# Sixty-four bytes of padding at the end of SBUF: where the right-hand tiles of an encoder layer begin

## The chip, the cores and the metric

The kernel runs on one core of a Trainium2 chip. A core has TensorE (PE in the profile, with its weight loads as PEld), VectorE (DVE), ScalarE (ACT), GpSimd (POOL) and SyncE (SP, which issues nearly all DMAs here). The engines work on SBUF, a memory of 128 partitions; TensorE writes its sums to PSUM. The metric is the device time of one execution in microseconds (us), the median over several runs.

## The reference, cut to what matters

One layer of a bidirectional encoder over 2048 tokens of width 1024, in float32:

```
h = rms_norm(x);  z = h @ w_in
y_a = mLSTM heads (chunks of 128, forward and backward scans) of z
y_b = latent attention, 4 heads, softmax over all 2048 keys, of z
x = x + concat(y_a, y_b) @ w_out
x = x + square(relu(rms_norm(x) @ w_ff1)) @ w_ff2        # 1024 -> 4096 -> 1024
```

## The kernel before

**Matmuls in three parts.** A float32 operand is split into a high and a low part of type float32r (names end in h and l), and a product is the sum of high x high, high x low and low x high. `mm3` (lines 68 to 71) issues these three matmuls. The first operand given to a matmul is the stationary one, loaded into TensorE before it; the second is the moving one, streamed through. The profile prints a matmul as out<-moving,stationary.

**Stages.** `phase_a` computes the norm, the input projection and what follows from it, and stores it to DRAM; a planner orders its instructions. From then on the order is written out by hand, and each engine runs its instructions in the order of the program:

- `attention` (line 989): blocks of 256 queries; for each half block and each 512 keys, a score group of five matmuls (lines 1075 to 1079), then softmax, transposes of the probabilities (line 1120) and the products with the values. The steps of the mLSTM are woven in between. `out` (line 1143) normalises a block into the tile y and stores it.
- `OutProj` (line 1288): the product with w_out, whose weights lie in the tiles woh0, wol0 and so on, with y as the stationary operand in ring tiles.
- `FeedForward` (line 1450). The first layer, `layer1`, uses a Strassen-like scheme: for each of 32 units (16 slices f of the hidden width, for each of 2 halves of the tokens), 7 products p of 12 matmuls each. `product` gives `mm3` the W1 combination wh, wl as the stationary operand, and the token combination `H[p]` as the moving one. The second layer, `layer2`, works in the same way with products pd.

**Where tiles lie.** Pools of tiles are taken from the left end of SBUF upwards, or with `side="right"` from the right end downwards; a pool that is closed gives its place to the next one. What matters here:

- Right, in this order from the end: `y_out` (line 998), which holds the one tile y; `stage` with eight raw tiles; then, in attention, the keys and queries (`k_sb`, `q_sb`), and in their place later `ring` (line 1315, tiles r), `o_w` (line 1316, the woh and wol), `f_h1` (the token combinations h3 to h6), and for the second layer `g_r` and `g_acc`.
- Left: the constants, the probabilities p, their transposes, the values, mLSTM tiles, later `f_h0` (the token combinations h0 to h2), `f_raw1` (W1 tiles w1raw) and the operands of the second layer.

All of these tiles but y and small ones of the mLSTM have a size that is a multiple of 128 bytes in each partition. So the size of y, which is opened first at the right end, sets where all the later right-hand tiles begin relative to such multiples.

**Which tiles a product meets.** For products 0 to 2 of units 1 to 11, `w1_split` (line 1497) puts the stationary W1 part into the left-hand w1raw tiles; in all other cases it goes into the right-hand ring:

```
if 0 < n < self.LOW and op < 3 and (n, op) != (1, 2):
    w = self.r1p.tile([P, 2, 4, P], F32R, name=f"w1raw{self.nlow % 2}")
else:
    w = self.ring.pool.tile([P, 2, 4, P], F32R, name="r0" if n or 2 < op < 6 else "r1")
```

The tokens of the first half are h0 to h6, for products 0 to 6. For the second half, `exchange` (line 1550) puts the tokens of product 0 into stage tiles (raw), those of product 1 into ring tiles (r), and those of products 2 to 6 into the places of h0 to h4.

Of the kernel before, what the change touches and what calls it, by code (L numbers as in the profile page):

```python
# [8 lines left out]
F32 = mybir.dt.float32  # L9
# [9 lines left out]
P = 128  # L19
# [969 lines left out]
def attention(c, keep, drain, project):  # L989

    nc, tc = c.nc, c.tc
    with ExitStack() as st:
        ent = st.enter_context
        skq, sl = ExitStack(), ExitStack()
        def pool(name, bufs, side="left", ent=ent, **kw):
            return ent(tc.tile_pool(name=name, bufs=bufs, side=side, reuse_waits="tile", **kw))

        op = pool("y_out", 1, "right", keep.enter_context)
# [143 lines left out]

        def out(b):
            h, blk = divmod(b, NB)
            y = op.tile([P, 264], F32, name="y")[:, 0:256]
            nc.vector.tensor_tensor(y, pvs.pop(b), dens.pop(b), op=ALU.mult)

            def store():
                nc.sync.dma_start(c.d_yb[h, :, blk * 256:(blk + 1) * 256], y)
            return store  # L1150
# [21 lines left out]
        for g in range(8 * N):  # L1172
# [4 lines left out]
            if r >= 0 and r % 8 == 6 and r // 8 < N:  # L1177
                out(r // 8)()
# [61 lines left out]
        invert(b)  # L1240
        transpose_group(b, 2, 0)
        out(b - 1)()
        transpose_group(b, 1, 1, True)
        pv(b, 0)
# [10 lines left out]
        next(after)  # L1255
        pv(b, 3)
        store = out(b)
        for _ in after:
            pass
# [751 lines left out]
```

## Time and profile before

| | us |
|---|---|
| median of 3 runs | 2583.69 (2583.47 to 2584.41) |
| profiled execution, first to last instruction | 2586.2 |
| TensorE busy in it | 2567.1 (99%) |
| VectorE | 1679.2 (65%) |
| ScalarE | 1211.0 (47%) |
| GpSimd | 402.9 (16%) |

No other time is given for the profiled execution than its span. In the span, `phase_a` takes about the first 460 us, attention with the mLSTM lasts until about 1155, the out-projection until 1348, the first feed-forward layer until 1972, and the second one until the end. A matmul is pipelined: a record lasts longer than the distance to the next one's start, so TensorE's rate is read from starts, and its busy share doesn't tell the rate.

### The profile page before, as it was taken

To read this page: it belongs to the slowest core of one execution; us is meant where nothing else is said; L and a number is where in the kernel's file an instruction comes from. 1 tells how busy PE (TensorE), PEld (TensorE's weight loads), DVE (VectorE), ACT (ScalarE), POOL (GpSimd) and SP (SyncE) were. 2 spreads that over 40 slices of the span, in tenths; PEclk is the share of its full clock that TensorE was granted. 3 is DMA by queue.
4 is the path that set the end of the run, shared out by engine and by line. 5 is a ranking of instruction groups with operands and counts; after the bars stand their busy time and mean duration, and the time that the engine had idled before them with its cause. 6 is when DMAs were issued, how large, how long until landed. Compare 5 with 4: busy or idle time off the path is not lost. (4 is left out here: it accounts for less than half of the span.)

```text
span 2586.2 us, 37106 instructions
## 1 busy us (share of the span) xinstructions
PE 2567.1 (99%) x13232; PEld 2170.3 (84%) x13232; DVE 1679.2 (65%) x3206; ACT 1211.0 (47%) x2457; POOL 402.9 (16%) x438
## 2 busy tenths in 40 slices
PE   9999999999999999999999999999999999999999
PEld 7888888888888888898888888888888888888887
DVE  5585467666676667675448777877775577676443
ACT  5454444546656566561135554655554323332332
POOL 1211111023224224121000000000000233232000
PEclk9999999999999999999999999999999999999999
DMA  5434234356455555336675655744446644444652
GB/s 172 144 118 143 91 119 145 81 137 133 96 95 122 88 119 96 88 109 185 200 242 174 200 192 191 255 167 143 163 142 250 242 144 146 147 147 147 211 177 96
DMA packets 297757, 391.57 MB, mean 151 GB/s; under 512 B 32677, under 2 KB 186340, under 8 KB 297572
## 3 DMA queue, kind: packets, MB, share of 16 engines
q1 hardware_dynamic: 295108, 384.74, 49.7%
q10 hardware_dynamic: 2464, 4.46, 0.5%
q8 instruction: 104, 1.70, 0.3%
q14 instruction: 81, 0.66, 0.1%
HBM read 256.94 MB, written 132.17 MB: 150 GB/s over the span
## 5 line engine op out<-in xcount | busy, mean ns | idle before, releaser
L69 PE MATMUL pd<-w2h,uh 128*128 128x512 f32 x896 | 348.7, 389 | 0.1
L71 PE MATMUL pd<-w2h,ul 128*128 128x512 f32 x896 | 348.6, 389 | 0.0
L70 PE MATMUL pd<-w2l,uh 128*128 128x512 f32 x896 | 348.5, 389 | 0.0
L54 DVE TENSOR_TENSOR ul<-ur,uh 128x1024 fp32r<-128x1024 f32 x110 | 144.4, 1312 | 248.7 <-ACT uh L53 248.4
L53 ACT CAST uh<-ur 128x1024 fp32r<-128x1024 f32 x110 | 115.9, 1054 | 395.5 <-PE pd L70 381.0
L54 DVE TENSOR_TENSOR ptl<-ptp,pth 128x512 fp32r<-128x512 f32 x252 | 173.5, 689 | 171.5 <-ACT pth L53 166.5
L53 ACT CAST pth<-ptp 128x512 fp32r<-128x512 f32 x252 | 146.3, 582 | 244.9 <-PE ptp L1120 228.6
L1629 DVE TENSOR_TENSOR e<-pu,e 128x512 f32<-128x512 f32 x224 | 151.0, 687 | 96.0 <-PE pu L71 94.0
L1080 DVE TENSOR_SCALAR_CACHE_REDUCE p<-ps 128x512 f32<-128x512 f32 x256 | 174.6, 682 | 53.5 <-PE ps L1079 42.6
L69 PEld LDWEIGHTS pd<-w2h,uh 128*128 128x128 f32 x896 | 168.2, 188 | 35.4 <-DVE e L1629 0.5
L71 PEld LDWEIGHTS pd<-w2h,ul 128*128 128x128 f32 x896 | 168.2, 188 | 35.0
L70 PEld LDWEIGHTS pd<-w2l,uh 128*128 128x128 f32 x896 | 168.2, 188 | 34.9
L1789 POOL TENSOR_TENSOR r<-wr,r 128x512 f32<-128x512 f32 x48 | 92.2, 1920 | 614.5 <-DMA wr<-in_w 599.2
L1120 PE MATMUL ptp<-ident,p 128*128 128x128 f32 x1008 | 151.3, 273 | 0.7 <-ACT p L1091 0.7
L69 PE MATMUL pz<-wh,hh 128*128 128x512 f32 (+1 forms) x384 | 149.9, 392 | 2.1 <-ACT hh L53 1.1
L71 PE MATMUL pz<-wh,hl 128*128 128x512 f32 (+1 forms) x384 | 150.3, 391 | 0.0
L70 PE MATMUL pz<-wl,hh 128*128 128x512 f32 (+1 forms) x384 | 149.7, 391 | 0.1
L70 PE MATMUL pv<-ptl,vh 128*128 128x256 f32 x496 | 140.8, 284 | 2.3 <-DVE ptl L54 1.9
L69 PE MATMUL pv<-pth,vh 128*128 128x256 f32 x496 | 140.6, 284 | 0.4 <-ACT pth L53 0.4
L71 PE MATMUL pv<-pth,vl 128*128 128x256 f32 x496 | 140.3, 283 | 0.0
L1632 ACT ACTIVATE e<-e 128x512 f32<-128x512 f32 x128 | 81.0, 633 | 124.0 <-DVE e L1629 117.2
L1091 ACT ACTIVATE p<-p,nm 128x2048 f32<-128x2048 f32 x64 | 128.6, 2009 | 20.8 <-DVE nm L1084 20.2
(470 smaller groups left out, 6561.8 us busy)
## 6 DMA issues: line engine op xcount, KB each, us to landing
d_u<-e SPq DMA_DIRECT2D x224, 256.0 KB
ur<-d_u SPq DMA_DIRECT2D x110, 512.0 KB
wr<-in_w SPq DMA_DIRECT2D x96, 256.0 KB
w1raw<-in_w SPq DMA_DIRECT2D x42, 512.0 KB
raw<-in_w_in SPq DMA_DIRECT2D x48, 256.0 KB
r<-in_w SPq DMA_DIRECT2D x22, 512.0 KB
mb<-d_M SPq DMA_DIRECT2D x32, 256.0 KB
r<-in_x SPq DMA_DIRECT2D x16, 512.0 KB
```

Source lines behind the costliest of these rows:

```text
L53: r = nc.scalar.copy(hi, src)
L54: (eng or nc.vector).tensor_tensor(lo, src, hi.bitcast(F32), op=ALU.subtract)
L69: nc.tensor.matmul(out, ah, bh, start=first, stop=False)
L70: nc.tensor.matmul(out, ah, bl, start=False, stop=False)
L71: nc.tensor.matmul(out, al, bh, start=False, stop=last)
L1080: nc.vector.tensor_scalar(probs[b, a][:, j, :], o, SCALE, None, op0=ALU.mult, op1=ALU.max, accum_out=maxes[b, a][:, j:j + 1])
L1091: nc.scalar.activation(p, p, AF.Exp, bias=maxes.pop((b, a)), accum_out=dens[b][:, a:a + 1])
L1120: nc.tensor.transpose(pt[:, k, :], p[:, j, k * P:(k + 1) * P], c.ident)
L1629: nc.vector.tensor_tensor(out, o, t, op=ALU.add)
L1632: nc.scalar.activation(t, t, AF.Relu)
L1789: nc.gpsimd.tensor_tensor(R, wr, R, op=ALU.subtract)
```

## The change

The tile y of an output block has 256 columns that are used and a padding behind them. The padding grows from 8 to 24 columns of 4 bytes:

```diff
         def out(b):
             h, blk = divmod(b, NB)
-            y = op.tile([P, 264], F32, name="y")[:, 0:256]
+            y = op.tile([P, 280], F32, name="y")[:, 0:256]
             nc.vector.tensor_tensor(y, pvs.pop(b), dens.pop(b), op=ALU.mult)
```

All right-hand tiles opened from then on begin 64 bytes further down in each partition, on multiples of 128 bytes. The instructions stay as they are.

## The prediction

> **What bounds the kernel now.** I read the page first, then TensorE's waits, then the stretches of the feed-forward layers, and then the matmuls one product at a time.
>
> ```profile
> span 2586.2 us, 37106 instructions
> ...
> PE 2567.1 (99%) x13232; PEld 2170.3 (84%) x13232; DVE 1679.2 (65%) x3206; ACT 1211.0 (47%) x2457; POOL 402.9 (16%) x438
> ```
>
> TensorE (PE) is busy for 2567.1 of 2586.2 us. Its longest wait is the first load of the kernel, and it is not touched here:
>
> ```profile
> PE pt L204 <- DMA rows<-in_g_mix: 4.6, 1, 4.6
> ```
>
> So the time is the sum of the matmuls' spacings, and a change to addresses can matter only if it changes a spacing or opens a wait. Busy time doesn't show spacings, because a matmul's record overlaps the next one. The stretches below are the first feed-forward layer in two halves (us; then PE, PEld, DVE, ACT, POOL busy with counts, clock, DMA share, GB/s):
>
> ```profile
> 1348.00:1660.00 312.00, 311.48 (x1398) 256.55 (x1397) 255.06 (x417) 168.04 (x302) 9.28 (x24) 1.00 0.62 203
> 1660.00:1972.00 312.00, 311.74 (x1358) 253.99 (x1357) 234.28 (x365) 166.71 (x269) 0.00 (x0) 1.00 0.47 158
> ```
>
> The granted clock is 1.00 in both, VectorE works 234.28/312 = 75% of the second, and the DMA engines 47%.
>
> The next view groups the matmuls of line 69, the first of the three in `mm3`. A name reads out<-moving,stationary; the three times are min/median/max of one matmul's duration in ns.
>
> ```profile
> L69 PE MATMUL pd<-w2h,uh x896: 389/389/494, 1971.9 to 2580.9; 128*128 128x512 f32 x180
> L69 PE MATMUL pv<-pth,vh x496: 277/283/384, 479.8 to 1149.1; 128*128 128x256 f32 x166
> ...
> L69 PE MATMUL po<-woh,r x256: 389/389/481, 1158.9 to 1347.2; 128*128 128x512 f32 x128
> ...
> L69 PE MATMUL pu<-h3h,r x128: 388/389/476, 1356.4 to 1968.5; 128*128 128x512 f32 x128
> L69 PE MATMUL pu<-h4h,r x128: 387/389/475, 1359.9 to 1971.3; 128*128 128x512 f32 x128
> L69 PE MATMUL pu<-h2h,r x88: 392/394/398, 1353.5 to 1965.8; 128*128 128x512 f32 x88
> L69 PE MATMUL pu<-h0h,r x84: 394/394/394, 1347.9 to 1960.2; 128*128 128x512 f32 x84
> L69 PE MATMUL pu<-h1h,r x84: 394/394/394, 1350.7 to 1963.0; 128*128 128x512 f32 x84
> L69 PE MATMUL pm<-wuqh,cTh x64: 334/337/343, 59.9 to 421.1; 128*128 128x384 f32 x64
> ...
> L69 PE MATMUL pu<-r,r x64: 389/389/389, 1665.3 to 1957.4; 128*128 128x512 f32 x64
> L69 PE MATMUL pu<-h0h,w1raw x44: 389/389/476, 1368.1 to 1566.5; 128*128 128x512 f32 x44
> ```
>
> Matmuls of one shape have two durations, and the odd ones are h0, h1 and h2 against the ring tile r: 394 ns instead of 389. Set the operands' places beside it. By the tile sizes in the code, h0 to h2 lie on the left side, on multiples of 128 bytes. The ring, h3 to h6 and the stage tiles lie on the right side, which now sits 64 bytes off such multiples. The same h0 against the left-hand w1raw takes 389; a right-hand moving tile (h3h, h4h, r) against the ring takes 389; pd, left against left, takes 389. So **both operands at the same distance from a multiple of 128 is the fast case; 0 against 64 is the slow one**.
>
> What it is worth is read from the timeline of one unit f of the second half, at the first matmul of a product (12 matmuls each):
>
> ```profile
> 1743.05 0.39 PE L69 MATMUL pu<-r,r 128*128 128x512 f32 x1
> ...
> 1745.77 0.39 PE L69 MATMUL pu<-h0h,r 128*128 128x512 f32 x1
> ...
> 1754.17 0.39 PE L69 MATMUL pu<-h3h,r 128*128 128x512 f32 x1
> ...
> 1756.91 0.39 PE L69 MATMUL pu<-h4h,r 128*128 128x512 f32 x1
> ```
>
> The product r,r takes 1745.77 - 1743.05 = 2.72 us (227 ns a matmul). The three products h0, h1, h2 take 8.40, which is 2.80 each (233 ns). The product h3 behind them takes 2.74: it needs 0.02 to find the fast rhythm again.
>
> **The change part by part.** The padded row grows from 264 x 4 = 1056 = 8 x 128 + 32 bytes to 280 x 4 = 1120 = 8 x 128 + 96. All right-hand tiles opened after it move down by 64 bytes, onto multiples of 128. No instruction, DMA or byte moved is added or taken away; nothing reads the padding.
>
> *1. The mismatched products, the main term.* The ring holds the stationary operand of h0, h1, h2 for 88 + 84 + 84 = 256 matmuls of line 69, and a product has four of these: 64 products. Each goes from 2.80 to 2.72 if all operands then sit at distance 0: 64 x 0.08 = **5.12 us**.
>
> *2. The products behind a change of distance.* h3 follows a mismatched product in units 12 to 31 (from 12 on, all W1 tiles come from the ring): 20 x 0.02 = **0.40 us**. In units 1 to 11 most of h0 to h2 go against w1raw, left against left, and h3 then changes over to right against right:
>
> ```profile
> 1550.84 0.39 PE L69 MATMUL pu<-h2h,w1raw 128*128 128x512 f32 x1
> ...
> 1553.56 0.39 PE L69 MATMUL pu<-h3h,r 128*128 128x512 f32 x1
> ...
> 1556.33 0.39 PE L69 MATMUL pu<-h4h,r 128*128 128x512 f32 x1
> ```
>
> h2 takes 2.72 and h3 2.77 here: 11 x 0.05 = 0.55, of which I take **0.50**, because the starts are rounded to 0.01.
>
> *3. Attention.* Keys and queries are both on the right and keep equal distances. But each score group stands between left-hand work (transposes of p, pv), so its edges change.
>
> ```profile
> 802.36 0.48 PE L1075 MATMUL ps<-kh,qh 128*128 128x512 f32 x1
> ...
> 803.37 0.39 PE L1079 MATMUL ps<-rl,qr 128*128 128x512 f32 x1
> ```
>
> Four matmuls take 1.01 us. There are 256 groups. The lower bound of the cost: the four matmuls behind the first come down from about 233 ns (the mismatched spacing) to 227, 4 x 0.0067 x 256 = 6.8 us gained. The upper bound: they lose a changeover of 0.01 (half of h3's 0.02), 256 x 0.01 = 2.6 us lost. The operands of a score match before and after, so I take **0**, and keep both ends.
>
> *4. What produces W1.* A unit of the second half then takes 7 x 2.72 = 19.04 us instead of 3 x 2.80 + 3 x 2.72 + 2.74 = 19.30. VectorE needs 75% of 19.30 = 14.5 us in it, ScalarE 53% = 10.3, so neither becomes the bound, and the matmuls hide them as before. Their own speed doesn't depend on the side:
>
> ```profile
> L47 DVE TENSOR_TENSOR r<-r,r 128x512 fp32r<-128x512 f32 x35 | 23.9, 684 | 1.1 <-ACT r L1505 1.1
> ...
> L47 DVE TENSOR_TENSOR w1raw<-r,w1raw 128x512 fp32r<-128x512 f32 x20 | 13.7, 683 | 0.0
> ```
>
> A row all on the right takes 684 ns, one across the sides 683: **0**. With no cover, 1 ns on each of the 365 VectorE operations of the second half would be 0.4 us. GpSimd does nothing in the second half.
>
> *5. Waits.* The 64 bytes move tile edges against tiles of earlier pools. By the sizes in the code, two edges that touched a weight slice of the opening stage no longer do, and the projection weight woh5 now touches the end of one mLSTM tile num1. It would wait for the last reader of num1:
>
> ```profile
> 1140.33 0.30 ACT L896 ACTIVATE num<-num 128x128 f32<-128x128 f32 x1
> L53 ACT CAST woh<-r x8: 627/632/637, 1159.0 to 1162.6; 128x512 fp32r<-128x512 f32 x8
> ```
>
> That ends at 1140.63, and the first cast from the ring, of which woh5 is one, comes at 1159.0: 18 us of cover, **0**. With the cover gone, whatever is late at ScalarE there delays the out-projection one for one.
>
> Sum: 5.12 + 0.40 + 0.50 = **6.0 us**. The profiled span is 2586.2, which is 2.5 above the runs' median of 2583.69; the profile has that on top, and the gain lies in spacings of an engine that never rests, so it comes off both: 2580.2 for the span and **2577.7 us** for the runs.
>
> **The rivals.**
>
> *No change (2583.7).* The 5 ns may belong to the sides being different, not to the 64 bytes. For it: every slow row has left moving and right stationary, and before shows no cross pair with equal distances in a long run. Against it: h3 lies right beside h2 and is fast, with the same ring; nothing but a 64-byte step is known to lie between them. The Trainium skill, TensorE: Matmul & The Clock Gate, section "Step-by-step: what each phase is for", speaks for this rival: TensorE has two independent read ports, so loading the next weights doesn't steal read bandwidth from the running matmul, and where operands lie could not matter. The trace disagrees with it so far: 394 against 389 ns.
>
> *Slower: the moving tile's own distance counts, wherever the stationary one is on the right.* h0 at 0 is slow and h3 at 64 fast against the same ring, which this explains as well as I do. Then h0 to h2 stay at 2.80, and the 128 fast ring products (of 224 products, 32 go against w1raw and 64 are slow already) and the out-projection (256 x 3 / 12 = 64 groups of twelve) all go to 2.80: (128 + 64) x 0.08 = 15.4 us, **2599.1**. It decides from 65 such groups on (65 x 0.08 = 5.2). Against it: wuqh with cTh, both on the right and on multiples of 128. From pd and pv a column costs (389 - 283)/256 = 0.41 ns, so 384 columns should take 389 - 53 = 336 in the fast class and 341 in the slow one; it takes 337.
>
> *Only the products (2578.6).* The changeovers stay, as they come from changing tiles: 2583.7 - 5.1.
>
> *Attention too (2570.9).* Step 3 at its lower bound, 2577.7 - 6.8.
>
> **How the numbers follow.** Chances: my forecast 0.66, only the products 0.10, attention too 0.08, no change 0.11, slower 0.05. A measurement of this kernel can tell about 0.2% (5.2 us) from no change. The forecast lies 0.8 us beyond that bound, "only the products" on it: I give it 0.03 faster, 0.07 same. Faster: 0.65 + 0.03 + 0.08 = 0.76; same: 0.11 + 0.07 = 0.18; slower 0.06 with what is left. The range takes in the forecast with some microseconds of step 3 to either side, and "only the products": 2573.0 to 2581.0. It leaves out no change, slower, and the far end of attention, about 0.2.
>
> **What would show it.** In the profile after: h0h,r to h2h,r at 389 ns like h3h,r, and a unit of the second half at 19.04 us (step 1); h3 at 2.72 in all units (step 2); score groups at 1.01 (step 3); VectorE and ScalarE rows of line 47 and 1505 unchanged (step 4); no new wait of TensorE near 1160 us (step 5). The forecast falls if h0h,r still shows 394, or if h3h,r or po rises to 394.

## The result, and the profile after

The changed kernel takes 2576.55 us (median of 9 runs, 2573.88 to 2577.52), the kernel before 2583.69 (9 runs): a ratio of 0.9971, with a 95% interval of 0.9962 to 0.9981. That is 7.1 us, where 6.0 were forecast. Instructions and counts are the same.

```profile
span 2575.0 us, 37106 instructions
...
PE 2557.5 (99%) x13232; PEld 2169.6 (84%) x13232; DVE 1675.9 (65%) x3206; ACT 1210.3 (47%) x2457; POOL 393.3 (15%) x438
```

The two profiled spans differ by 11.2 us, more than the medians. The execution profiled before lay some 4 us above the median of the runs: a span here is 1.8 us shorter than the device time of its execution (2576.82 for 2575.0), so 2586.2 stands for about 2588. I therefore compare stages, and take totals from the ratios.

The first feed-forward layer, in the view of the matmuls of line 69 (min/median/max ns, first and last start):

```profile
L69 PE MATMUL pu<-h3h,r x128: 387/389/476, 1350.4 to 1957.4; 128*128 128x512 f32 x128
L69 PE MATMUL pu<-h4h,r x128: 388/389/476, 1354.2 to 1960.1; 128*128 128x512 f32 x128
L69 PE MATMUL pu<-h2h,r x88: 389/389/389, 1347.6 to 1954.7; 128*128 128x512 f32 x88
L69 PE MATMUL pu<-h0h,r x84: 389/389/389, 1342.2 to 1949.2; 128*128 128x512 f32 x84
L69 PE MATMUL pu<-h1h,r x84: 389/389/389, 1344.9 to 1951.9; 128*128 128x512 f32 x84
```

The 394 ns of h0, h1 and h2 have become 389. In the timeline, the same unit as shown of before:

```profile
1737.73 0.39 PE L69 MATMUL pu<-h0h,r 128*128 128x512 f32 x1
...
1745.89 0.39 PE L69 MATMUL pu<-h3h,r 128*128 128x512 f32 x1
...
1748.61 0.39 PE L69 MATMUL pu<-h4h,r 128*128 128x512 f32 x1
```

The three products take 8.16 us, 2.72 each, and the h3 behind them 2.72 too. From the first matmul of this layer to the first of the next, the layer now takes 1960.8 - 1342.2 = 618.6 us. Before, it took 1971.9 - 1347.9 = 624.0.

That is 5.4 us, not 6.0, because two waits of this layer grew:

```profile
PE pu L71 <- DVE r L47: 0.7, 1, 0.7
...
PE pu L70 <- DVE h4l L47: 0.6, 1, 0.6
```

They were 0.5 and 0.3 before. With the slower start behind them (the timeline shows h3 of unit 0 at 3.77 us against 3.55 before, and h4 of unit 16 at 3.65 against 3.27) they give back 0.6 us. TensorE seems to come to them earlier than VectorE can deliver.

Attention gained as well, which I had not counted. Before, by the groups of the score matmuls (busy us, mean ns of one):

```profile
L1078 PE MATMUL ps<-rh,qr 128*128 128x512 f32 x256 | 101.6, 397 | 0.0
...
L1079 PE MATMUL ps<-rl,qr 128*128 128x512 f32 x256 | 101.3, 396 | 0.0
```

and after:

```profile
L1078 PE MATMUL ps<-rh,qr 128*128 128x512 f32 x256 | 100.9, 394 | 0.0
L1079 PE MATMUL ps<-rl,qr 128*128 128x512 f32 x256 | 100.5, 392 | 0.0
```

The records of the last two matmuls of a group are 3 and 4 ns shorter. What attention gained by it is tried below, with kq192.

### The profile page after: what moved, and what is told of

Its sections match the earlier page's. It is cut to its first block, busy times and chain, and to the rows that moved or that the text cites. A ratio compares the mean times of both kernels' runs of the same rounds, so it can differ in the third digit from the quotient of the medians.

```text
span 2575.0 us, 37106 instructions
## 1 busy us (share of the span) xinstructions
PE 2557.5 (99%) x13232; PEld 2169.6 (84%) x13232; DVE 1675.9 (65%) x3206; ACT 1210.3 (47%) x2457; POOL 393.3 (15%) x438
## 5 line engine op out<-in xcount | busy, mean ns | idle before, releaser
L1789 POOL TENSOR_TENSOR r<-wr,r 128x512 f32<-128x512 f32 x48 | 82.8, 1725 | 619.1 <-DMA wr<-in_w 599.1
```

What stands on the lines that cost most here:

```text
L1789: nc.gpsimd.tensor_tensor(R, wr, R, op=ALU.subtract)
```

## The experiments

My theory, A: a matmul pays 6.7 ns when its moving and its own stationary tile begin at different places modulo 128. Its rivals were B, that multiples of 128 are fast wherever the other operand lies, and C, that moving tile edges, and not alignment, did it. In each run the sum of the three products h0 to h2 against the ring in one unit of the second half (unit 20 of before and after, 21 of the others) tells what a slow product costs: 8.40 us before, 8.16 after. Ratios are against the kernel before, run on the same chip.

**left64: the old padding, the left side moved instead.**

```diff
-        c.e = ep.tile([P, 12, 512], F32, name="e")
+        c.e = ep.tile([P, 12 * 512 + 16], F32, name="e")[:, 0:12 * 512].rearrange("p (a n) -> p a n", a=12)
```

> Padding as before (264 columns), but 64 bytes of padding behind the left-hand tile e, so that h0 to h2, the w1raw tiles and the second layer's operands begin 64 bytes off multiples of 128, as the right-hand tiles do. Theory A (a matmul pays 6.7 ns when its moving and its own stationary tile begin at different places modulo 128): every product of the first feed-forward layer takes 2.72 us, as after, and the changeovers vanish; about 6.0 us faster than before, near 2577.7; attention stays as before. Theory B (multiples of 128 are what is fast, wherever the other operand lies): h0 to h2 against the ring stay at 2.80, and h0 to h2 against w1raw and all of pd may join them; no gain or a loss, 2583.7 or more.

Ratio 0.9977 (0.9968 to 0.9987).

```profile
1761.32 0.39 PE L69 MATMUL pu<-h0h,r 128*128 128x512 f32 x1
...
1769.48 0.39 PE L69 MATMUL pu<-h3h,r 128*128 128x512 f32 x1
```

8.16 us: all products are fast with every tile of these products 64 bytes off a multiple of 128. B falls, and so does the reading that the multiples themselves are what the change brings. The layer takes 618.5 us, as after. The ratio alone tells less: its interval, 3.4 to 8.3 us, holds the expected 6.0 and the 7.1 of the change.

**both: the new padding and the left side moved.** The edit of left64 on the changed kernel, so that left and right lie 64 bytes apart again, the other way round.

> Padding as after (280 columns) and the 64 bytes behind e as well: right-hand tiles on multiples of 128, left-hand feed-forward tiles 64 off. Theory A: the slow products come back, h0 to h2 against the ring at 2.80 us, 64 x 0.08 + 0.9 = 6.0 us slower than after, near 2582.5; the gain of attention stays. Theory B: the ring and h3 to h6 are on multiples of 128, so they are fast; h0 to h2 are off them, so they are slow both against the ring and against w1raw: 96 products at 2.80. The rows tell the two apart: h0h against w1raw takes 389 ns by A and 394 by B.

Ratio 0.9986 (0.9977 to 0.9995).

```profile
1759.90 0.40 PE L69 MATMUL pu<-h0h,r 128*128 128x512 f32 x1
...
1768.16 0.40 PE L69 MATMUL pu<-h3h,r 128*128 128x512 f32 x1
...
1770.93 0.39 PE L69 MATMUL pu<-h4h,r 128*128 128x512 f32 x1
```

```profile
L69 PE MATMUL pu<-h0h,w1raw x44: 389/394/477, 1363.9 to 1562.3; 128*128 128x512 f32 x44
L69 PE MATMUL pu<-h1h,w1raw x44: 389/389/476, 1366.6 to 1565.0; 128*128 128x512 f32 x44
```

By the sign set beforehand, h0h against w1raw at 394 would speak for B. But B has all of h0 to h2 slow against w1raw, and h1h takes 389: left against left is fast, and h0h is the first product after a change of sides. Left against right is slow again, but costs less: 8.26 us for three products instead of 8.40, and 2.77 for the h3 behind. A forecast 8.40. It has no place for this: 0 against 64 and 64 against 0 are the same distance modulo 128.

**pad272 and pad256: right-hand tiles 32 and 96 off.**

```diff
-            y = op.tile([P, 280], F32, name="y")[:, 0:256]
+            y = op.tile([P, 272], F32, name="y")[:, 0:256]
```

(256 in the second.)

> 272 columns: all right-hand tiles 32 bytes off multiples of 128, left-hand ones on them. Theory A in its strict form (any difference costs the same): h0 to h2 against the ring at 2.80 us, as before, near 2583.7. Theory A with 64-byte halves (only the 64 counts): 2.72 us, near 2576.6 as after. A cost that grows with the distance would give about 2.76 us, near 2580. Theory C (what the change did was to move tile edges, not alignment) expects a time anywhere between.

> 256 columns, no padding: all right-hand tiles 96 bytes off multiples of 128, that is 32 below them, left-hand ones on them. Theory A in its strict form: 2.80 us for h0 to h2 against the ring, near 2583.7. With 64-byte halves: 96 counts as 64, 2.80 us, near 2583.7. With the distance to the nearest multiple of 128 counting: as for 272 columns.

Ratios 0.9992 (0.9983 to 1.0001) and 0.9998 (0.9989 to 1.0007).

```profile
1763.09 0.40 PE L69 MATMUL pu<-h0h,r 128*128 128x512 f32 x1
...
1771.49 0.39 PE L69 MATMUL pu<-h3h,r 128*128 128x512 f32 x1
```

```profile
1765.28 0.40 PE L69 MATMUL pu<-h0h,r 128*128 128x512 f32 x1
...
1773.71 0.40 PE L69 MATMUL pu<-h3h,r 128*128 128x512 f32 x1
```

8.40 and 8.43 us: the whole price for 32 as for 96. It neither grows with the distance nor comes in halves of 64.

**pad296 and pad312: further down.** These separate places modulo 128 (A1) from the signed distance over a longer stretch (A2).

```diff
-            y = op.tile([P, 280], F32, name="y")[:, 0:256]
+            y = op.tile([P, 296], F32, name="y")[:, 0:256]
```

(312 in the second.)

> 296 columns: right-hand tiles once more 64 bytes off multiples of 128, but 128 bytes further down than in before. Theory A1 (the places modulo 128 decide, moving at 0 and stationary at 64 being the dear order and moving at 64 with stationary at 0 the cheaper one): h0 to h2 against the ring at 2.80 us as before, ratio near 1.000. Theory A2 (the signed distance over a longer stretch, modulo 256, decides: the moving tile began 64 below the stationary one in before and 64 above it in both, and here it is 64 above it): 2.76, 2.75, 2.75 and 2.77 us for h0, h1, h2 and the h3 behind them, as in both, ratio near 0.999. Theory C (tile edges or room): neither of the two patterns.

> 312 columns: right-hand tiles on multiples of 128 as after, but 128 bytes further down, so that left and right differ by 128 modulo 256. Theory A1: everything as after, all products at 2.72 us, ratio near 0.997. Theory A2: a distance of 128 is a distance like another, h0 to h2 against the ring above 2.72.

Ratios 0.9982 (0.9973 to 0.9991) and 0.9986 (0.9977 to 0.9995).

```profile
1766.63 0.40 PE L69 MATMUL pu<-h0h,r 128*128 128x512 f32 x1
...
1774.89 0.40 PE L69 MATMUL pu<-h3h,r 128*128 128x512 f32 x1
```

```profile
1767.16 0.40 PE L69 MATMUL pu<-h0h,r 128*128 128x512 f32 x1
...
1775.56 0.39 PE L69 MATMUL pu<-h3h,r 128*128 128x512 f32 x1
```

With 296 columns the right side lies 64 off multiples of 128, just as in before, and yet the three products take 8.26 us as in both. With 312, **every tile of these products lies on a multiple of 128 and they are slow again, 8.40 us**. A1 falls twice; A2 stands. C falls too: the patterns follow the distances.

**pad344 and pad288: how long is the stretch, and does the sign count?** The same edit with 344 and 288 columns.

> 344 columns: right-hand tiles 256 bytes further down than after. Theory A2 (the signed distance of the moving tile's begin from the stationary one's decides, modulo some length; 0 is the only fast one so far, and 128 is slow): if the length is 256, every product takes 2.72 us again, ratio near 0.997. If it is 512 (the step between two slices of a stationary tile, so it cannot be longer), 256 is one more slow distance, h0 to h2 against the ring above 2.72, ratio near 0.999.

> 288 columns: right-hand tiles 32 bytes further down than after, the moving tiles h0 to h2 begin 32 above the stationary ones (modulo 256). Theory A2: plus 64 cost 2.75 to 2.77 us, minus 32 cost 2.80. If the sign is what makes the difference, plus 32 lies between 2.72 and 2.77, ratio near 0.998. If every distance but plus 64 costs the same, 2.80, ratio near 1.000.

Ratios 0.9978 (0.9968 to 0.9987) and 0.9993 (0.9984 to 1.0002).

```profile
1760.75 0.39 PE L69 MATMUL pu<-h0h,r 128*128 128x512 f32 x1
...
1768.91 0.39 PE L69 MATMUL pu<-h3h,r 128*128 128x512 f32 x1
```

```profile
1763.24 0.40 PE L69 MATMUL pu<-h0h,r 128*128 128x512 f32 x1
...
1771.64 0.40 PE L69 MATMUL pu<-h3h,r 128*128 128x512 f32 x1
```

With 256 more bytes the products are fast, 8.16 us: the stretch is 256. With a distance of 32 in the other direction they cost 8.40, so the sign alone doesn't make a product cheap; plus 64 is the one distance tried that is cheaper. Together, with places from the layout of the program:

| moving (left) minus stationary (right), modulo 256 | three products, us | from |
|---|---|---|
| 0 | 8.16 | after, left64, pad344 |
| +32 | 8.40 | pad288 |
| +64 | 8.26 | both, pad296 |
| 128 | 8.40, 8.39 | pad312, ident64 |
| -96 | 8.43 | pad256 |
| -64 | 8.40 | before |
| -32 | 8.40 | pad272 |

**kq64 and kq192: attention's share.** Both are the changed kernel with a gap that moves only keys and queries.

```diff
         rp = pool("stage", 8, "right", keep.enter_context)
+        pool("gap", 1, "right", skq.enter_context).tile([P, 48], F32, name="gap")
         kp = pool("k_sb", 5, "right", skq.enter_context)
```

(16 columns in kq64.)

> Padding as after (280 columns), but 64 bytes of padding between the stage tiles and the keys and queries, so that only keys and queries lie 64 bytes off again, as in before; all of the feed-forward layers as after. If keys and queries on multiples of 128 are what shortens attention, the score groups go back to their spacings of before (the four matmuls behind the first 1.3 + 0.7 + 0.5 us in total longer) and the time is about 2 us longer than after, ratio near 0.998. If attention's share in the gain is chance (waits of one execution), the time is that of after, ratio near 0.997.

kq64 has a ratio of 0.9972 (0.9961 to 0.9984), as the changed kernel, and its last two score rows show 394 and 393 ns, as after. By its expectation attention's share would be chance. But by the stretch of 256 it hadn't restored the old places: keys and queries lay 64 below the left side's places, not 64 above them. Hence kq192, with the changed kernel once more beside it (again):

> Padding as after, and 192 bytes between the stage tiles and the keys and queries, which puts these at the same places modulo 256 as in before; all else as after. If attention's share of the gain comes from where keys and queries lie, the matmuls behind the first of a score group go back to their spacings of before, and the time is about 2 us above that of the same kernel without the gap, in the run beside it. If not, both agree within 0.5 us.

> The changed kernel once more, beside the others, as what kq192 is compared with: ratio near 0.997, attention's score groups as in the profile after.

kq192 takes 2583.34 us (0.9983, 0.9975 to 0.9992) and the changed kernel 2580.98 (0.9973, 0.9963 to 0.9982). That is 2.4 us. The intervals overlap, but 9 of the 11 executions of kq192 took longer than every one of the 9 of the changed kernel. The score groups of kq192, one line number higher, are those of before, 397 and 396 ns:

```profile
L1079 PE MATMUL ps<-rh,qr 128*128 128x512 f32 x256 | 101.6, 397 | 0.0
L1080 PE MATMUL ps<-rl,qr 128*128 128x512 f32 x256 | 101.3, 396 | 0.0
```

and those of the changed kernel beside it are short again:

```profile
L1078 PE MATMUL ps<-rh,qr 128*128 128x512 f32 x256 | 101.0, 395 | 0.0
L1079 PE MATMUL ps<-rl,qr 128*128 128x512 f32 x256 | 100.4, 392 | 0.0
```

Records don't tell the rate, so I add up the distances from start to start of the 1280 score matmuls, short waits included: 324.3 us in kq192 against 322.3 in again, and 323.6 in before against 321.3 in after. That is 2.0 and 2.3 us. The whole stretch from the first score to the first projection matmul can't be used for this. It takes 713.0 us in kq192 and 710.7 in again, which looks like the difference of the medians, but 707.2 in after, which is the same kernel as again: waits there differ by some microseconds from one execution to the next. So attention's share follows where keys and queries lie, and its size, about 2 us, is less sure than that of the feed-forward layer. The two placements that differ by 128 bytes, kq64 and kq192, do not act alike here either.

**ident64: can the transposes' settling be shortened?** After transposes, matmuls take 231 to 236 ns for a while before they run at 227. Here the identity, their moving operand, moves by 64 bytes on the changed kernel:

```diff
-    c.ident = pool.tile([P, P], F32, name="ident")
+    c.ident = pool.tile([P, P + 32], F32, name="ident")[:, 16:P + 16]
```

> Padding as after, but the identity matrix, the moving operand of all transposes, lies 64 bytes off a multiple of 128, and everything on the left side behind it 128 bytes higher. Theory A1: the feed-forward products stay at 2.72 us; the transposes have moving at 64 and stationary at 0. If the distance also sets how long the matmuls behind transposes take to settle (231 to 236 ns instead of 227 for up to ten matmuls), the score groups change by up to 0.02 us each, 5 us in all, either way; if it does not, the time is that of after.

Ratio 0.9987 (0.9978 to 0.9996), slower than the changed kernel.

```profile
1766.82 0.40 PE L69 MATMUL pu<-h0h,r 128*128 128x512 f32 x1
...
1775.21 0.39 PE L69 MATMUL pu<-h3h,r 128*128 128x512 f32 x1
```

The loss is in the feed-forward layer: the left side moved by 128 with the identity, and the three products take 8.39 us, as in pad312. So A1 falls here a third time. The four score rows behind the first of a group show 394 to 395 ns, against 392 to 396 after: nothing was won there. No version tried beats the changed kernel.

## Why the prediction was right or wrong

*Direction and size were right*: 7.1 us (4.9 to 9.8 by the interval) against 6.0, the time 1.1 below the forecast and inside the range. That the total came so near is helped by two terms taken as 0, attention's gain and the waits of step 4, which went opposite ways.

*Step 1, the mismatched products*: as forecast, 8.40 to 8.16 us for three, 64 products by 0.08. In the traces these 64 took 179.2 us before and 174.2 after. left64 shows it without the change: matching the sides from the left gives the same product times.

*Step 2, the changeovers*: as forecast. h3 takes 2.72 after h2, where it took 2.74.

*Step 3, attention, taken as 0*: this is the term that was mis-sized. It is about 2 us gained (2.4 by the medians of kq192 and the changed kernel, 2.0 to 2.3 by the starts), inside the bounds of 6.8 gained and 2.6 lost. The step named the left-hand work around a group but took it for nothing, because the operands of a score match before and after. In the traces the matmuls behind the first of a group lie 232 to 236 ns apart in the median before and 230 to 233 after, not at the steady 227. That what stands around so short a group sets this is inferred; only the place of keys and queries was tried. Why some matmuls of a group gain and others don't was not shown.

*Step 4, taken as 0*: 0.6 us was given back, though neither VectorE nor ScalarE became the bound of a unit. The two waits were short before (0.5 and 0.3 us) and belong to single places, the weights of unit 0 and h4 for the second half; a mean load of 75% doesn't show them. That their suppliers kept their pace while TensorE came sooner is inferred, not tried by itself. It fits that left64, which speeds up the same products in another way, shows the same waits, 0.7 and 0.6 us.

*Step 5, waits from moved edges*: no wait of TensorE above 0.15 us in the profile after was new; the woh5 edge cost nothing.

*The rule behind it was wrong in its form.* "0 against 64 bytes from a multiple of 128 is the slow one" described the rows of before, which held only one slow distance. What counts is the distance of the moving tile's begin from the stationary one's, modulo 256. pad312 puts every tile of these products on a multiple of 128 and is as slow in them as before. The change works because the left side happened to lie at 128 modulo 256 and the right side came to lie there too. That was luck: the rule as forecast would have promised the same of 312 columns, which cost 8.40 us. So the words "on multiples of 128" name neither what is needed (left64) nor what is enough (pad312).

*The rivals.* No change, and slower by the moving tile's own distance, both fell: h0h is at 389 ns, and h3h and h4h did not rise. The row held against the second, wuqh with cTh, was misread: by the layout its two tiles begin 128 apart modulo 256. Its 337 ns for 384 columns lies between the 336 reckoned for fast and the 341 for slow. So the price for shorter matmuls is not known from these runs. Only the products fell with step 2. Attention too was right in kind, at about a third of the price given. The Trainium skill, TensorE: Matmul & The Clock Gate, section "Step-by-step: what each phase is for", holds that weight loads don't steal read bandwidth from the running matmul; read as the rival read it, no product could have changed. Here the same matmul's spacing ran from 227 to 234 ns with nothing changed but the two operands' places (8.16 and 8.43 us for 36).

*Open:* whether the stationary tile that counts is the matmul's own or the next one's, which is loaded while it runs. In a steady row both lie alike. The places where two products meet tell them apart in part. In pad272 and pad288 the last matmul of h6 always has its own stationary tile at distance 0. It takes 226 or 227 ns when the next matmul's stationary tile lies in the ring, and 235 in the median when that lies in w1raw, on the other side. So there the next tile counts. pad256, pad312 and ident64 show the same, with medians of 232 to 236. But in before, both and pad296, at distances of 64, that matmul takes 226 and only those behind it are slow. Whether the own tile counts as well stays open, and so does the mechanism: the runs show only what the price depends on.

## What to carry to other kernels

Where TensorE bounds and matmuls of one shape show two durations, group them by the pair of tiles and set the tiles' addresses beside it: here, with 512 columns, the moving and the stationary tile had to begin at the same place modulo 256 bytes, and which of the two places tried (128 and 192) made no difference. A small odd-sized tile at the outer end of one side shifts all tiles behind it, so such a tile sets the distance between the two sides for the whole kernel. Read the gain from spacings of starts, and look for short waits just behind: 0.6 us of 6.0 went into them.

## What the runs showed of the hardware that was not expected

The price is nearly a step: distances of 32, 64, 96 and 128 cost 6.7 to 7.5 ns a matmul alike ((8.40 - 8.16)/36 and (8.43 - 8.16)/36), in both signs where both were tried at 32. Only plus 64 was cheaper, 2.8 ns ((8.26 - 8.16)/36), and there part of it comes late: the h3 behind takes 2.77 us, where it took 2.74 in before and 2.72 after. These are means. From start to start the price comes in a pattern that each distance has for itself: with 312 columns the matmuls take 229 and 237 or 238 ns in turn, and in both 232, 226 and 229.
